# Output stores moved from SyncE to ScalarE and head sums a slot later, in a layer of two token mixers

## The chip, the cores and the metric

The kernel runs on one core of one Trainium2 chip. The metric is the device time of one execution in microseconds, the median of several runs. The engines are named as the profile names them: PE is TensorE (PEld its weight loads), DVE is VectorE, ACT is ScalarE, POOL is GpSimd and SP is SyncE, which here only issues DMAs. DMAs can be issued from SyncE's queue (SPq) or from ScalarE's (ACTq).

## The reference

2048 tokens of 1024 features go through one layer. Cut to what matters:

```python
xn = rms_norm(x, ln_g)
proj = einsum('bsd,de->bse', xn, w_in)
b_gate, c_gate, x_conv, g_conv, x_lru, g_lru = split(proj)      # 1024 columns each
y_conv = short_conv_mixer(b_gate, c_gate, x_conv, conv_w)
y_conv = headwise_rms_norm(y_conv, 8, conv_out_g) * silu(g_conv)
y_lru = rg_lru_mixer(x_lru, ...)                                # gated linear recurrence
y_lru = headwise_rms_norm(y_lru, 16, lru_out_g) * silu(g_lru)
y = concatenate([y_conv, y_lru])                                # 2048 features
h = x + einsum('bse,ed->bsd', y, w_out)
out = rms_norm(h, final_g)
```

The two head-wise norms need, for each token and head, the sum of squares over the head's features: these are the "head sums". The output projection is a product of 2048 features by 1024 columns, and the residual add and the last norm follow row by row.

## The kernel before

**How the products are made.** Every matrix is kept as a high and a low part (`sh`, `sl` for the streaming side, `th`, `tl` for the weights), and each product is three matmuls: `mm` (L877 issues them) takes high by high, high by low and low by high. A Strassen-like scheme needs seven products of half blocks where the plain way takes eight. One half-block product is four chunks `j` of three matmuls, so 12 matmuls of 128x512; such a group is called a **slot** here, and seven (sometimes eight) slots make a **step**. There are 48 steps for the input projection (half `h` of the tokens 0 or 1, block `k` from 0 to 7, and the kinds "l", "a" and "b") and 16 steps "o" for the output projection: phase `ph` 0 and 1, pair of row blocks `m` from 0 to 7.

**What sets the order.** The order is that of the code, engine by engine. `tick()` is called once at the start of each slot; `at(n, f)` puts `f` down to be run `n` ticks later, and whatever it issues stands at that place in the streams of all engines it uses. So "a slot later" means: the instruction stands behind twelve more matmuls on PE, and behind whatever the other engines were given in that slot. Each engine works through its own stream in order, and an instruction that waits holds back all behind it, a DMA issue on SP too.

**The head sums.** `finish` (L560 to L587) is called at the end of a mixer's block. It multiplies with the gate and the gain (`f1`, L565), stores the result to DRAM (`store`, L570), squares it on ScalarE, makes a high part `qh` there (L576) and a low part `ql` on VectorE, and then `head_sums` (L546 to L558) adds up the squares over the features of each head by four small matmuls with a selection matrix `sel`, into the PSUM tile `norm_ps`. After the last block `head_norms` makes the reciprocal roots and stores them (`rsd`). `hl_done(2)` gives two of four tiles of the pool "hl" back to a count, on which a background job (`jobs`, with `may`) hangs: that job prepares the sets `so` of the output projection's streaming side (a ScalarE cast at L417, a VectorE subtraction, a store to DRAM at L422) and the sums `traw` of blocks of `w_out` (loads at L381, stores at L395). Such a job goes on by a piece when the count allows.

**The input projection's copies.** PSUM banks are freed by ScalarE copies: `q` (L1208), `u` (L1211) and `rr` (L1214) take the first three products of a step, and VectorE combines them with later banks. In the kinds "l" ScalarE also starts the convolution, `u<-xl` at L631.

**The output projection.** `outp` (L793 on) makes, for each pair, two row blocks `i` = 0 and 1 of 128 tokens. In phase 0 the first 1024 features of `y` are used: a residual block `xr` is loaded from `x` (L803), the product `ob` added to it on VectorE, and the sum stored to a scratch array `od` in DRAM (L813). In phase 1 the other 1024 features are used: `xr` is loaded back from `od`, added, the row's sum of squares taken on ScalarE (L819) and its root (L820), the block scaled on VectorE (`f2`, L824) and stored to `out` (`f3`, L828). The last block of all (`m` = 7, `i` = 1) goes in two halves (L833 to L841), one store from SP and one from ACT. The weights of a phase are a set of 28 tiles `th`/`tl`; between the phases the second set is loaded (`traw`, L446) and split while the matmuls go on. The streaming sides `s<-so` are loaded at L218.

Of the kernel before, what the change touches and what calls it, by code (L numbers as in the profile page):

```python
# [17 lines left out]
P = 128  # L18
# [20 lines left out]
def hymba_kernel(ctx: ExitStack, tc: tile.TileContext, x, xt, w_in, par, lamc, w_gate, w_out, final_g, out):  # L39
    nc = tc.nc  # L40
# [19 lines left out]
    od = [dram.tile([P, D], F32, name=f"od{b}") for b in range(S // P)]  # L60

    def wt(tag, name, n=2 * C, dt=F32, bufs=1):
        return work.tile([P, n], dt, tag=tag, bufs=bufs, name=name)
# [77 lines left out]
    def at(slots, *fs):  # L141
        if slots == 0:
            for f in fs:
                f()
        else:
            due.append([slots, fs])
# [12 lines left out]
    def tt(out, a, b, op, eng=None):  # L159
        (eng or nc.vector).tensor_tensor(out=out, in0=a, in1=b, op=op)  # L160
# [176 lines left out]
    def hl_tile(name, n=1):  # L337
        hlc[0] += n
        return [wt("hl", name, dt=F32R, bufs=HL) for _ in range(n)]

    def hl_done(n):
        hlc[0] -= n
# [126 lines left out]
    def rstd(rs, ss):  # L469
        nc.scalar.activation(out=rs, in_=ss, func=AF.Sqrt, scale=1.0 / D, bias=eps)  # L470
        nc.vector.reciprocal(out=rs, in_=rs)
# [63 lines left out]
    def head_norms(h):  # L535
        rs = aux("hn")[:R]
        nc.scalar.activation(out=rs, in_=norm_ps[0], func=AF.Sqrt, scale=inv_hd, bias=eps[:R])
        at(1, lambda: nc.vector.reciprocal(out=rs, in_=rs))

        def store():  # L540
            for i in range(2):
                nc.sync.dma_start(rsd[2 * h + i].rearrange("b h t -> h b t"),
                                  rs[32 * i:32 * i + 3 * KT, :].rearrange("h (b t) -> h b t", b=NB))
            normed.extend([h] * h)

        at(3, store)  # L546

    def head_sums(h, qh, ql, col, row):
        if norm_ps[1] == 0:
            norm_ps[0] = psn.tile([P, C], F32, tag="norm", name="norm_ps")[:R]  # L550
        for i in range(2):
            s0 = col - (32 * i + row)
            for q in (qh, ql):
                nc.tensor.matmul(norm_ps[0], sel[:, s0:s0 + R], q[:, i * C:(i + 1) * C],  # L554
                                 start=norm_ps[1] == 0, stop=norm_ps[1] == 8 * KT - 1)
                norm_ps[1] += 1
        if norm_ps[1] == 8 * KT:
            norm_ps[1] = 0  # L558
            at(1, lambda: head_norms(h))

    def finish(d0, h, kt, y, sil, gain, col, row):
        v = {}

        def f1():
            nc.vector.scalar_tensor_tensor(out=sil, in0=y, scalar=gain, in1=sil,  # L565
                                           op0=ALU.mult, op1=ALU.mult)

        def store():
            for i in range(2):
                nc.sync.dma_start(yd[2 * h + i][:, :, kt, :].rearrange("b p t -> p b t"),  # L570
                                  sil[:, i * C:(i + 1) * C].rearrange("p (b t) -> p b t", b=NB))

        def f2():
            nc.scalar.activation(out=y, in_=y, func=AF.Square)
            v["qh"], = hl_tile("qh")
            nc.scalar.copy(v["qh"], y)  # L576

        def f3():
            v["ql"], = hl_tile("ql")
            tt(v["ql"], y, v["qh"].bitcast(F32), ALU.subtract)  # L580

        at(d0, f1)
        at(d0 + 2, store)
        at(d0 + 2, f2)
        at(d0 + 3, f3)
        at(d0 + 6, lambda: head_sums(h, v["qh"], v["ql"], col, row))
        at(d0 + 7, lambda: hl_done(2))  # L587

    def silu(g, late=0):
        sg = [None]  # L590
# [28 lines left out]
    def lru(h, k, late=0):  # L619
# [80 lines left out]
        def out_():  # L700
            finish(0, h, KT + k, v["r"], g, pt[:, LG + k:LG + k + 1], 2 * R, KT + k)
# [20 lines left out]
    def combine(dst, bank, other):  # L722
        if other is None:
            nc.scalar.copy(dst, bank)
        else:
            tt(dst, bank, other, ALU.add)
# [66 lines left out]
    def outp(ph, m):  # L793
        ob = [wt("hl", "ob", bufs=HL) for _ in range(2)]
        xr = {}
        if ph == 1 and m == 0:
            fg[0] = wt("t", "fg")
            nc.sync.dma_start(fg[0], final_g.rearrange("(o d) -> o d", o=1).broadcast_to((P, D)))

        def load(i):  # L800
            tb = 2 * m + i
            xr[i] = wt("ig", "xr", bufs=IG) if i == 0 else wt("o2", "xr", bufs=O2)
            nc.sync.dma_start(xr[i], x[tb * P:(tb + 1) * P, :] if ph == 0 else od[tb])  # L803

        last = ph == 1 and m == KT - 1
        at(2 if last else 5, lambda: load(0))
        at(2 if last else 6, lambda: load(1))

        def fin(i):
            tb = 2 * m + i  # L810
            if ph == 0:
                at(1, lambda: tt(xr[i], xr[i], ob[i], ALU.add))
                at(3, lambda: nc.sync.dma_start(od[tb], xr[i]))  # L813
                return
            ss = small.tile([P, 2], F32, tag="ss", bufs=4, name="ss")
            rs = small.tile([P, 1], F32, tag="rs", bufs=4, name="rs")

            def f1():
                nc.scalar.activation(out=xr[i], in_=ob[i], func=AF.Square, accum_out=rs)  # L819
                nc.scalar.activation(out=rs, in_=rs, func=AF.Sqrt, scale=1.0 / D, bias=eps)  # L820

            def f2():
                nc.vector.reciprocal(out=rs, in_=rs)
                nc.vector.scalar_tensor_tensor(out=ob[i], in0=ob[i], scalar=rs, in1=fg[0],  # L824
                                               op0=ALU.mult, op1=ALU.mult)

            def f3():
                nc.sync.dma_start(out[tb * P:(tb + 1) * P, :], ob[i])  # L828

            if last and i == 1:  # L830
                for d in (1, 0):
                    ds_ = slice(d * C, (d + 1) * C)
                    nc.scalar.activation(out=xr[i][:, ds_], in_=ob[i][:, ds_], func=AF.Square,  # L833
                                         accum_out=ss[:, d:d + 1])
                tt(rs, ss[:, 0:1], ss[:, 1:2], ALU.add)
                rstd(rs, rs)
                for d in range(2):
                    ds_ = slice(d * C, (d + 1) * C)
                    nc.vector.scalar_tensor_tensor(out=ob[i][:, ds_], in0=ob[i][:, ds_], scalar=rs,
                                                   in1=fg[0][:, ds_], op0=ALU.mult, op1=ALU.mult)  # L840
                    (nc.sync, nc.scalar)[d].dma_start(out[tb * P:(tb + 1) * P, ds_], ob[i][:, ds_])  # L841
                return
            if last:
                tt(ob[i], ob[i], xr[i], ALU.add)
                f1()
                f2()
                f3()
                return
            at(1, lambda: tt(ob[i], ob[i], xr[i], ALU.add))
            at(3, f1)  # L850
            at(4, f2)
            at(5, f3)

        def put(which, bank, other):
            i, d = which // 10 - 1, which % 10 - 1
            ds_ = slice(d * C, (d + 1) * C)
            if last and i == 1 and d == 0:
                tt(xr[i][:, ds_], xr[i][:, ds_], other, ALU.add)
                combine(ob[i][:, ds_], bank, xr[i][:, ds_])
            else:  # L860
                combine(ob[i][:, ds_], bank, other)
                if last and i == 1:
                    tt(ob[i][:, ds_], ob[i][:, ds_], xr[i][:, ds_], ALU.add)
            if which == 12:
                fin(0)
            if which == 21:
                fin(1)

        return put
# [41 lines left out]
    with tc.manual_schedule(engines={ENG.PE, ENG.Activation, ENG.DVE, ENG.Pool, ENG.SP}):  # L911
# [173 lines left out]
        for n in range(PLAIN, N):  # L1085
            kind, h, k = steps[n]
# [52 lines left out]
            for s in range(8 if new or last else 7):  # L1139
                i = ((0, 6) + ORDER[1:])[s]  # L1140
# [131 lines left out]
```

## Time and profile before

| | us |
|---|---|
| median of 3 runs | 1426.95 |
| lowest and highest | 1425.71, 1427.22 |
| the profiled execution | 1426.31 |
| its span | 1424.5 |
| PE busy in it | 1335.4 |
| mean granted clock in it | 0.982 of full speed |

The rows of the timeline give the start, the duration, the engine, the line, the operation, the output and input names, and in brackets how long the engine had been idle before it and what ended that. Rows with "x2" join neighbours of one kind. The stages in the table by windows are: a step of the input projection (783 to 841), phase 0 of the output projection without its beginning (1125 to 1253), the passage to phase 1 (1253 to 1282) and phase 1 (1282 to 1405); the rest to 1424.5 is the last block and its norm.

### The profile page before, as it was taken

Reading aid. Unit: us, or ns where it says so; the run is one execution under the profiler, and the core shown is the slowest. Engines: PE = TensorE matmul, PEld = TensorE weight load, DVE = VectorE, ACT = ScalarE, POOL = GpSimd, SP = SyncE. Lnnn points to the kernel's source line nnn. Section 1 sums busy time; section 2 is a strip of 40 time slices with the busy share of each in tenths; the row PEclk is TensorE's granted clock in tenths of the full one; section 3 lists DMA queues with packets and bytes.
Section 4 is the critical chain, followed back from the end, with each engine's and each line's share of the span. In section 5 each row is a group of like instructions: output and inputs, shape, how many; then the busy total and the mean of one; then the engine's idle time right before and its main releaser. Section 6 shows DMA issues by size and latency. Waiting matters only on the chain.

```text
span 1424.5 us, 16977 instructions
## 1 busy us (share of the span) xinstructions
PE 1335.4 (94%) x5732; PEld 1068.4 (75%) x5732; DVE 1069.8 (75%) x1264; ACT 782.0 (55%) x1165; POOL 258.4 (18%) x168
## 2 busy tenths in 40 slices
PE   5979999999999997899998999899996999989997
PEld 4867777778787775677886878687874788868885
DVE  5788887998989889777767667665657548668885
ACT  6576668566665756475563645463646323434442
POOL 2414343434534331001000000101010000000000
PEclk9999999999999998999999999999998999989999
DMA  5137797987978866631899999998978999698643
GB/s 212 30 110 259 271 275 239 284 322 273 328 275 297 305 246 220 225 102 38 276 313 339 332 342 326 347 315 307 288 269 330 348 292 278 215 403 292 216 156 122
DMA packets 165190, 371.02 MB, mean 260 GB/s; under 512 B 17264, under 2 KB 52464, under 8 KB 165104
## 3 DMA queue, kind: packets, MB, share of 16 engines
q1 hardware_dynamic: 164672, 369.63, 75.7%
q8 instruction: 45, 0.74, 0.2%
q14 instruction: 41, 0.34, 0.1%
q10 hardware_dynamic: 432, 0.32, 0.1%
HBM read 224.45 MB, written 145.43 MB: 260 GB/s over the span
## 4 chain that ended last, share of the span: by engine, by line
PE 63%; DVE 11%; DMA 10%; ACT 10%; issue 3%; SPq 2%; POOL 0%; DVEq 0%; ACTq 0%
PE bank L877 59%; DVE s L160 2%; ACT i L668 2%; PE gate L661 2%; DMA traw<-in_w_out_dram 2%; ACT r L668 2%; PE norm_ps L554 2%; DVE tl L160 2%; DMA sd<-s 1%; DVE traw L160 1%; DVE r L695 1%; DMA zr<-rsd 1%; DMA so<-so 1%; DMA s<-sd 1%; ACT q L1208 1%
## 5 line engine op out<-in xcount | busy, mean ns | idle before, releaser
L877 PE MATMUL bank<-th,s 128*128 128x512 f32 x3608 | 1145.6, 394 | 43.1 <-DMA s<-so 8.8
L877 PEld LDWEIGHTS bank<-th,s 128*128 128x128 f32 x3608 | 683.4, 189 | 207.5 <-issue 14.5
L877 PE MATMUL bank<-tl,s 128*128 128x512 f32 x1804 | 709.7, 393 | 7.1 <-DVE tl L160 6.5
L877 PEld LDWEIGHTS bank<-tl,s 128*128 128x128 f32 x1804 | 341.7, 189 | 83.2 <-DVE tl L160 11.7
L160 POOL TENSOR_TENSOR s<-raw,s 128x512 fp32r<-128x512 f32 x67 | 127.2, 1911 | 263.2 <-ACT s L197 217.1
L197 ACT CAST s<-raw 128x512 fp32r<-128x512 f32 x136 | 81.9, 617 | 56.9 <-PE bank L877 39.8
L1211 ACT COPY u<-bank 128x512 f32<-128x512 f32 x58 | 34.0, 587 | 140.1 <-PE bank L877 90.2
L160 POOL TENSOR_TENSOR gb<-gb,sg 128x1024 f32<-128x1024 f32 x16 | 42.5, 2658 | 352.4 <-ACT sg L594 296.1
L160 DVE TENSOR_TENSOR s<-s,s 128x512 fp32r<-128x512 f32 x102 | 100.6, 986 | 5.4 <-ACT s L197 5.4
L160 DVE TENSOR_TENSOR tl<-traw,th 128x512 fp32r<-128x512 f32 x98 | 66.5, 705 | 46.9 <-ACT th L454 29.4
L160 DVE TENSOR_TENSOR s<-raw,s 128x512 fp32r<-128x512 f32 (+1 forms) x115 | 86.6, 777 | 9.9 <-ACT s L197 5.3
L1208 ACT COPY q<-bank 128x512 f32<-128x512 f32 x58 | 33.8, 583 | 83.0 <-PE bank L877 75.8
L160 DVE TENSOR_TENSOR raw<-raw,zr 128x512 f32<-128x512 f32 x64 | 47.9, 769 | 36.8 <-DMA zr<-rsd 36.8
L197 ACT CAST s<-s 128x512 fp32r<-128x512 f32 x102 | 62.8, 616 | 7.5 <-DVE s L160 7.4
L635 DVE SCALAR_TENSOR_TENSOR u<-xl,pt,u 128x1024 f32<-128x1024 f32 x48 | 65.4, 1363 | 0.7 <-ACT u L631 0.2
L1214 ACT COPY rr<-bank 128x512 f32<-128x512 f32 x58 | 33.9, 584 | 45.7 <-PE bank L877 45.6
L745 DVE SCALAR_TENSOR_TENSOR t<-p,pt,t 128x1024 f32<-128x1024 f32 x32 | 48.5, 1517 | 4.9 <-ACT t L742 4.1
L160 DVE TENSOR_TENSOR st<-u,st 64x1024 fp32r<-64x1024 f32 x32 | 50.9, 1590 | 1.0
L160 POOL TENSOR_TENSOR gl<-gl,sg 128x1024 f32<-128x1024 f32 x16 | 45.6, 2849 | 14.4 <-ACT sg L594 14.4
L631 ACT ACTIVATE u<-xl,pt 128x1024 f32<-128x1024 f32 x16 | 19.9, 1246 | 48.1 <-DVE xl L160 48.0
L160 DVE TENSOR_TENSOR ob<-bank,rr 128x512 f32<-128x512 f32 x18 | 12.2, 689 | 44.7 <-ACT rr L1214 44.7
L668 ACT ACTIVATE r<-gate,pt 64x512 f32<-64x512 f32 x64 | 43.7, 683 | 1.7 <-PE gate L661 1.1
(161 smaller groups left out, 1372.2 us busy)
## 6 DMA issues: line engine op xcount, KB each, us to landing
sd<-s SPq DMA_DIRECT2D x147, 512.0 KB, 4.8
s<-sd SPq DMA_DIRECT2D x147, 512.0 KB, 6.0
raw<-in_w_in_dram SPq DMA_DIRECT2D x108, 256.0 KB, 4.7
so<-so SPq DMA_DIRECT2D x42, 512.0 KB, 6.2
s<-so SPq DMA_DIRECT2D x42, 512.0 KB, 7.5
raw<-yd SPq DMA_DIRECT2D x64, 256.0 KB, 5.8
traw<-in_w_out_dram SPq DMA_DIRECT2D x56, 256.0 KB, 5.9
yd<-gl SPq DMA_DIRECT2D x32, 256.0 KB, 3.7
```

Of the source, the lines that this page charges most:

```text
L160: (eng or nc.vector).tensor_tensor(out=out, in0=a, in1=b, op=op)
L197: nc.scalar.copy(dst[i][0], val(i))
L554: nc.tensor.matmul(norm_ps[0], sel[:, s0:s0 + R], q[:, i * C:(i + 1) * C], start=norm_ps[1] == 0, stop=norm_ps[1] == 8 * KT - 1)
L631: nc.scalar.activation(out=v["u"], in_=o1[:, 1:1 + N2], func=AF.Identity, scale=lw[0], bias=pt[:, LB + k:LB + k + 1])
L635: nc.vector.scalar_tensor_tensor(out=v["u"], in0=o1[:, 1 + j:1 + j + N2], scalar=lw[j], in1=v["u"], op0=ALU.mult, op1=ALU.add)
L661: nc.tensor.matmul(ps[j], v["gw"][n][:, j, :], v["st"][j][:, sl], start=(n == 0), stop=(n == 1))
L668: nc.scalar.activation(out=g_[hi, sl], in_=v["ps"][j][src], func=AF.Sigmoid, bias=pt[src, bias + k:bias + k + 1])
L745: nc.vector.scalar_tensor_tensor(out=tcur["t"], in0=p[:, 2 + j:2 + j + N2], scalar=cw[j], in1=tcur["t"], op0=ALU.mult, op1=ALU.add)
L877: nc.tensor.matmul(bank, a[:, js], b, start=start and n == 0, stop=stop and n == 2, skip_group_check=more)
L1208: nc.scalar.copy(q1, bk["A"])
L1211: nc.scalar.copy(u2, bk["A"])
L1214: nc.scalar.copy(rr, bk["A"])
```

## The change

`head_sums` and the `hl_done` behind it come a slot later in every call of `finish`. The stores of phase 0 (16, of 512 KB) and of phase 1 (15, of 512 KB) are issued by ScalarE instead of SyncE, and each a slot later: three slots after the add in phase 0, two slots after the scaling in phase 1. In the last step `f3` is called at once, without `at`, and now goes to ScalarE too.

```diff
@@ finish
-        at(d0 + 6, lambda: head_sums(h, v["qh"], v["ql"], col, row))
-        at(d0 + 7, lambda: hl_done(2))
+        at(d0 + 7, lambda: head_sums(h, v["qh"], v["ql"], col, row))
+        at(d0 + 8, lambda: hl_done(2))
@@ outp, fin
-                at(3, lambda: nc.sync.dma_start(od[tb], xr[i]))
+                at(4, lambda: nc.scalar.dma_start(od[tb], xr[i]))
...
-                nc.sync.dma_start(out[tb * P:(tb + 1) * P, :], ob[i])
+                nc.scalar.dma_start(out[tb * P:(tb + 1) * P, :], ob[i])
...
-            at(5, f3)
+            at(6, f3)
```

Three places show it in the streams. The first is on PE, in a step "l" of the second half, at 774 us of the trace. `norm_ps` are the head sums with `qh` and `ql` (two more, alike, follow the two shown), `bank_6456` and `bank_6354` two PSUM banks, `th` weights and `s` streaming sides. Before:

```order
L877 MATMUL bank_6456<-th_4878,s_6332 128x512
L554 MATMUL norm_ps_5465<-qh_6370,sel_177 64x512
L554 MATMUL norm_ps_5465<-ql_6403,sel_177 64x512
...
L877 MATMUL bank_6354<-th_4743,s_6330 128x512
L877 MATMUL bank_6354<-tl_4744,s_6330 128x512
...
L877 MATMUL bank_6354<-th_4904,s_6330 128x512
L877 MATMUL bank_6456<-th_4626,s_6352 128x512
```

The same place after the change:

```order
L877 MATMUL bank_6456<-th_4878,s_6332 128x512
L877 MATMUL bank_6354<-th_4743,s_6330 128x512
L877 MATMUL bank_6354<-tl_4744,s_6330 128x512
...
L877 MATMUL bank_6354<-th_4904,s_6330 128x512
L554 MATMUL norm_ps_5493<-qh_6370,sel_177 64x512
L554 MATMUL norm_ps_5493<-ql_6403,sel_177 64x512
...
L877 MATMUL bank_6456<-th_4626,s_6352 128x512
```

The head sums have moved behind the twelve matmuls into `bank_6354`, to directly before the first matmul that writes `bank_6456` again. All 32 groups have moved in the same way.

The second place is on ACT, in the last steps of phase 0 and the passage to phase 1, from 1237 to 1255 us in the trace before: the stores of row blocks 12 to 15 among the copies that free banks (`u`, `rr`, `ob`) and the casts of the weights of phase 1 (`th<-traw`).

```order
 L454 CAST th<-traw 128x512 x2
 L197 CAST s<-raw 128x512
-L1211 COPY u_10035<-bank 128x512
+L1211 COPY u_10034<-bank 128x512
+L813 DMA od_148<-xr 128x1024
 L454 CAST th<-traw 128x512 x4
 L1214 COPY rr<-bank 128x512
+L813 DMA od_149<-xr 128x1024
 L454 CAST th<-traw 128x512 x4
 L724 COPY ob<-bank 128x512
-L454 CAST th<-traw 128x512 x18
+L454 CAST th<-traw 128x512 x4
+L813 DMA od_150<-xr 128x1024
+L813 DMA od_151<-xr 128x1024
+L454 CAST th<-traw 128x512 x14
```

`od_148` to `od_151` are the stores of row blocks 12 to 15; the last two stand next to each other. On SP the same four stores are gone from between the loads of `s<-so` and `traw`.

The third place is on ACT at the end of the program: the copies and norms of the last pair of row blocks.

```order
 L820 ACTIVATE rs<-rs,eps 128x1
 L1214 COPY rr<-bank 128x512
-L724 COPY ob<-bank 128x512
-L819 ACTIVATE xr,rs<-ob 128x1024
-L820 ACTIVATE rs<-rs,eps 128x1
+L828 DMA out_dram<-ob 128x1024
+L724 COPY ob<-bank 128x512
+L819 ACTIVATE xr,rs<-ob 128x1024
+L820 ACTIVATE rs<-rs,eps 128x1
+L828 DMA out_dram<-ob 128x1024 x2
 L833 ACTIVATE xr,ss<-ob 128x512 x2
 L470 ACTIVATE rs<-rs,eps 128x1
```

Two stores (row block 14, called at once, and block 13, two slots behind its scaling) now stand between the root of block 14 and the two squares of block 15 (L833).

## The prediction

> **What bounds the kernel now.** The first page of the profile gives the span and each engine's share of it.
>
> ```profile
> span 1424.5 us, 16977 instructions
> PE 1335.4 (94%) x5732; PEld 1068.4 (75%) x5732; DVE 1069.8 (75%) x1264; ACT 782.0 (55%) x1165; POOL 258.4 (18%) x168
> ```
>
> TensorE is busy for 94% of the span. So an edit is worth what it does to TensorE's waits, or to TensorE's rate. The profiled execution took 1426.31 us: 1.8 us lie around its span, and it stands 0.6 us under the median of 1426.95 us. I add my terms to the median. About 0.2% (2.9 us) is what a measurement of this kernel can tell from no change.
>
> Next I read the list of what TensorE waits for, and then the same table for SyncE's DMA queue.
>
> ```profile
> PE bank L877 <- DMA s<-so: 8.8, 5, 3.3
> PE bank L877 <- ACT q L1208: 6.0, 5, 1.4
> PE norm_ps L554 <- DVE ql L160: 5.5, 4, 1.4
> PE bank L877 <- DMA s<-sd: 4.6, 6, 1.0
> ```
>
> ```profile
> SPq L828 <- DVE ob L824: 67.4, 15, 13.6
> SPq L813 <- DVE xr L160: 26.5, 7, 7.1
> ```
>
> The columns are microseconds in all, times, and the longest. The third row of the first table is the wait of the head sums, which the change moves: 5.5 us in four pieces. The two rows below are the waits of the stores that leave SyncE. They are large, but they are waits of a queue, and cost time only where a load behind them comes late for TensorE. Whether one does is read from the busy time by stages: TensorE, its weight loads, VectorE, ScalarE, GpSimd, then granted clock, DMA share and GB/s.
>
> ```profile
> core 0: us, PE busy (x) PEld busy (x) DVE busy (x) ACT busy (x) POOL busy (x), PEclk, DMA share, GB/s
> 783.00:841.00 58.00, 56.49 (x246) 45.38 (x244) 36.50 (x42) 31.09 (x42) 6.31 (x4) 1.00 0.97 339
> 1125.00:1253.00 128.00, 128.00 (x565) 105.67 (x564) 78.30 (x108) 39.78 (x69) 0.00 (x0) 1.00 0.86 279
> 1253.00:1282.00 29.00, 23.14 (x81) 17.74 (x80) 16.33 (x25) 11.04 (x19) 0.00 (x0) 0.82 1.04 401
> 1282.00:1405.00 123.00, 123.00 (x543) 101.55 (x542) 100.53 (x148) 56.66 (x109) 0.00 (x0) 1.00 0.63 214
> ```
>
> The output projection runs from about 1105 us. In 1125 to 1253 (phase 0) and 1282 to 1405 (phase 1) TensorE has no idle time at all. So in 251 of its 320 us the stores and their waits cost nothing today. Only the passage between the phases (1253 to 1282) has idle time and a lowered clock.
>
> **The head sums, a slot later.** I take the first of the four waits apart in the timeline. TensorE:
>
> ```profile
> 774.25 0.40 PE L554 MATMUL norm_ps<-qh,sel 128*64 128x512 f32 x1
> 776.02 0.45 PE L554 MATMUL norm_ps<-ql,sel 128*64 128x512 f32 x1 [1.38 <-DVE ql L160]
> 781.09 0.50 PE L877 MATMUL bank<-th,s 128*128 128x512 f32 x1 [1.41 <-ACT q L1208]
> ```
>
> VectorE and ScalarE in the same stretch:
>
> ```profile
> 774.14 0.69 DVE L160 TENSOR_TENSOR gl<-bank,rr 128x512 f32<-128x512 f32 x1 [6.33 <-DMA yd<-gl]
> 774.75 1.22 DVE L160 TENSOR_TENSOR ql<-r,qh 128x1024 fp32r<-128x1024 f32 x1
> 778.54 0.68 DVE L160 TENSOR_TENSOR xl<-bank,q 128x512 f32<-128x512 f32 x1
> 779.33 1.24 ACT L631 ACTIVATE u<-xl,pt 128x1024 f32<-128x1024 f32 x1 [8.11 <-DVE xl L160]
> 780.47 0.56 ACT L1208 COPY q<-bank 128x512 f32<-128x512 f32 x1
> ```
>
> VectorE stands 6.33 us before `gl` until an earlier store has landed, and everything behind it is late: first `ql`, on which the head sums wait 1.38 us, and then without a pause `xl`, ScalarE's `u` and, queued behind `u`, the copy `q`, which frees the PSUM bank that TensorE wants at 781.09 (again a wait, 1.41 us). Nothing in this second chain depends on the head sums. After the change the twelve matmuls that stood behind the head sums run at 774.25 and the head sums follow, with `ql` (ready at 775.97) no longer waited for. But the bank still comes at 781.09. So the 1.38 us are given back 5 us later, as one gap of 1.38 + 1.41 = 2.8 us. Two more of the four sites have the same second gap:
>
> ```profile
> 846.65 0.50 PE L877 MATMUL bank<-th,s 128*128 128x512 f32 x1 [1.39 <-ACT q L1208]
> 913.26 0.50 PE L877 MATMUL bank<-th,s 128*128 128x512 f32 x1 [1.41 <-ACT q L1208]
> ```
>
> The fourth (974 us) shows no wait of TensorE at its `q`; there up to 1.4 us might stay won, but the weight load stands there already, so I count nothing. Term: 0, bounds -1.4 and 0. The other 28 groups of head sums wait for nothing and only change places.
>
> A gap of 2.8 us is another thing than two of 1.4, since the clock answers to gaps. I look for gaps of nearby size in the timeline of TensorE.
>
> ```profile
> 568.78 0.49 PE L877 MATMUL bank<-th,s 128*128 128x512 f32 x1 [2.06 <-ACT th L277]
> 578.15 0.74 PE L877 MATMUL bank<-th,s 128*128 128x512 f32 x1 [2.57 <-ACT th L277]
> 579.47 1.05 PE L877 MATMUL bank<-th,s 128*128 128x512 f32 x2
> 581.86 0.63 PE L877 MATMUL bank<-th,s 128*128 128x512 f32 x2
> 1254.59 0.47 PE L877 MATMUL bank<-th,s 128*128 128x512 f32 x1 [0.85 <-DMA s<-so]
> 1257.23 0.54 PE L877 MATMUL bank<-th,s 128*128 128x512 f32 x1 [1.71 <-DVE tl L160]
> 1275.42 0.76 PE L877 MATMUL bank<-th,s 128*128 128x512 f32 x1 [3.30 <-DMA s<-so]
> 1281.47 0.63 PE L877 MATMUL bank<-th,s 128*128 128x512 f32 x2
> ```
>
> After 2.06 us of idleness the next matmul takes 0.49 us; after 2.57 and 3.30 us it takes 0.74 and 0.76, and two overlapped ones take 1.05 us where they take 0.63 at full rate. From 578.15 to 581.86 eight matmuls pass in 3.71 us, which need 8 x 0.23 = 1.84 at the full spacing (0.23 us is what a second, overlapped matmul adds: two take 0.63, the single one at 774.25 took 0.40): 1.9 us lost. From 1275.42 to 1281.47 fourteen matmuls lose 6.05 - 3.22 = 2.8 us. Three gaps of 2.8 us, then, above the 2.57 that drops the clock, at 1.9 each: +5.7 us, bounds 0 (no drop) and 3 x 2.8 = 8.4. Part of it is taken back, where TensorE waited for DMA loads between the sites: in that stretch the DMA share is 0.97 (the row of 783 to 841), so a later TensorE finds these loads landed. The `s<-sd` row above holds 4.6 us in all; I let half of the loss be absorbed: +2.9.
>
> [...]
>
> On TensorE, at the first of these sites, the order before has the four head sums (`norm_ps`) ahead of the twelve matmuls into the other bank, and after the change behind them; nothing else moves there. Loads of `xcol` and `xrow` on SyncE that wait for the head sums (in the first 300 us) go 2.7 us later, ahead of a use several microseconds away: 0. Since `hl_done` comes later too, six of the background splits `so` (a ScalarE cast and a VectorE subtraction) stand one slot later and four sets of `w_out` loads two loads later on SyncE. No row of TensorE's waits shows these at the places concerned; I count 0, with 1 us to either side in the range.
>
> **The stores on ScalarE.** One issue costs about the same on either queue:
>
> ```profile
> L828 SPq DMA_DIRECT2D out_dram<-ob x15: 333/338/338, 1292.5 to 1417.0; - x15
> L813 SPq DMA_DIRECT2D od<-xr x16: 319/330/911, 1117.9 to 1257.2; - x16
> 1421.30 0.35 ACTq L841 DMA_DIRECT2D out_dram<-ob x1
> ```
>
> 31 issues x 0.35 = 10.9 us come onto ScalarE. In the two steady stages it works 39.8 + 56.7 = 96 of 251 us, so they hide there; a slot (about 2.7 us) is left between VectorE's result and the store, so ScalarE should hardly wait for VectorE, which would hold back the copies behind the store that free TensorE's banks. SyncE loses its two waits of 67.4 and 26.5 us, but TensorE was waiting for nothing behind them in these stages: 0, not a gain.
>
> What is left is the passage, where TensorE waits for loads that SyncE issues:
>
> ```profile
> 1253.24 0.32 SPq L813 DMA_DIRECT2D od<-xr  x1
> 1254.52 0.32 SPq L218 DMA_DIRECT2D s<-so  x1
> 1268.70 3.09 SPq L218 DMA_DIRECT2D s<-so  x5
> ```
>
> The passage moves 401 GB/s at a DMA share of 1.04: it is bound by transfers. A store of 512 KB takes 0.512 MB / 401 GB/s = 1.3 us of it. The stores of blocks 12 and 13 go some 4 us later, out of a lull before 1235 us into the full time, and those of 14 and 15 stand together on ScalarE at about 1254, on a queue of their own beside the loads. That costs from one to two stores' time, 1.3 to 2.6 us, when the next load is the one TensorE waits for; the third gap, 3.30 us at 1275.42, hangs on loads issued only at 1268.70 and need not move. On the other side the issues leave SyncE's way (0.3 us each) and the loads queued behind them may go earlier: down to -3. I take +1, bounds -3 and +4.
>
> [...]
>
> **The end.** ScalarE now issues the last store of block 14 ahead of its last squares:
>
> ```profile
> 1415.67 1.28 DVE L824 SCALAR_TENSOR_TENSOR ob<-ob,rs,fg 128x1024 f32<-128x1024 f32 x1
> 1415.34 0.61 ACT L833 ACTIVATE xr<-ob 128x512 f32<-128x512 f32 x1
> 1418.38 0.63 ACT L833 ACTIVATE xr<-ob 128x512 f32<-128x512 f32 x1 [2.34 <-DVE ob L160]
> ```
>
> It waits there for VectorE until 1416.95, and two issues of 0.35 us follow (block 13's stands behind it), so the first square starts at about 1417.7 and ends at 1418.5, where the second was to begin at 1418.38: +0.1 to +0.6, taken +0.3.
>
> **The sum.** 0 + 2.9 + 1.0 + 0.3 = +4.2 us on 1426.95: 1431.1, called 1431.0.
>
> **The rivals.** First, no drop of the clock: the merged gaps of 2.8 us fall so that the rate stays full, as after 2.06 us. Then 0 + 0 + 1.0 + 0.3: 1428.3 us, no measurable change. For it: the edge lies between 2.06 and 2.57, and near the edge a gap's place may decide.
>
> Second, faster: SyncE, free of 94 us of waits, feeds the passage earlier. Its three gaps (0.85, 1.71 and 3.30 us) and the 2.8 us lost at half rate behind the last are worth 8.7 us. It decides once the loads land about 1 us sooner: then the last gap falls under the edge of 2.57 us, and I put half of the sum, 4.4 us, as gone: 1426.95 - 4.4 + 0.3 = 1422.9 us if the clock holds at the head-sum sites. Against it: the passage is already full of transfers.
>
> Third, the change of the head sums costs nothing, but blocks 14 and 15 on the second queue hold back the loads of the passage by 2.6 us, and a gap there crosses the edge (1.9 us): 1426.95 + 4.5 + 0.3 = 1431.8. Against it: the third gap takes up part of a delay.
>
> That the change does not do what it says has no chance here: the order has all 32 groups and 31 stores in other places.
>
> **How the numbers follow.** Forecast 0.48, no clock drop 0.27, faster 0.17, transfers 0.08. Of the forecast's case 0.06 falls within 2.9 us of the median, and of the second rival's 0.04 as well when the drop takes part of its gain back; of the no-drop case 0.06 goes below and 0.02 above. Faster: 0.13 + 0.06 = 0.19. Same: 0.06 + 0.19 + 0.04 = 0.29. Slower: 0.42 + 0.02 + 0.08 = 0.52. The forecast's own range is 1428 to 1437: its upper end has the clock's loss unabsorbed (5.7) and the transfers' upper bound (4). For 8 in 10 the lower end goes down to 1423.0, the price of the faster rival, which leaves out its better half.
>
> **What would show it.** Right: TensorE's waits for `ql` at 776, 842, 908 and 974 us gone, a single wait of about 2.8 us for `q` at three of them, then matmuls of 0.74 us and a granted clock under 1.00 for 3 to 6 us; no idle TensorE in the two steady stages; DMA still full in the passage. The no-drop rival: the same gaps, followed by 0.50 us. Wrong: the `q` wait stays at 1.4 us, so that 5.5 us are won; or TensorE waits in the steady stages for copies held behind a store on ScalarE.

## The result and the profile after

The changed kernel takes 1437.31 us (median of four runs, 1435.67 to 1441.15) against 1426.97 us before (four runs, 1425.71 to 1427.22). The ratio is 1.0075 with a 95% interval of 1.0059 to 1.0090: slower by 10.7 us (8.4 to 12.8). The forecast was 1431.0 us with a range up to 1437.0; the direction was right, and the predicted rise of 4.2 us was less than half of what came. The profiled execution is the slowest of the four (1441.15 us, span 1439.2), so its gaps make more than the median shows.

First, where the time went. The copy `rr` (L1214) is made once a step, so the same copy can be looked up in both traces. These are the 30th, 42nd, 45th and last of 58, before:

```profile
763.91 0.59 ACT L1214 COPY rr<-bank 128x512 f32<-128x512 f32 x1
1027.98 0.59 ACT L1214 COPY rr<-bank 128x512 f32<-128x512 f32 x1
1128.47 0.59 ACT L1214 COPY rr<-bank 128x512 f32<-128x512 f32 x1 [5.82 <-PE bank L877]
1406.64 0.59 ACT L1214 COPY rr<-bank 128x512 f32<-128x512 f32 x1 [3.48 <-PE bank L877]
```

and after:

```profile
764.87 0.59 ACT L1214 COPY rr<-bank 128x512 f32<-128x512 f32 x1
1034.70 0.59 ACT L1214 COPY rr<-bank 128x512 f32<-128x512 f32 x1
1141.67 0.59 ACT L1214 COPY rr<-bank 128x512 f32<-128x512 f32 x1 [4.86 <-PE bank L877]
1421.29 0.59 ACT L1214 COPY rr<-bank 128x512 f32<-128x512 f32 x1 [3.48 <-PE bank L877]
```

The lag is 1.0 us at the first, 6.7 at the second, 13.2 at the third and 14.65 at the last. So of the 14.7 us of this pair of executions, 5.8 arise in the stretch with the four head-sum sites, 6.5 from there into the first steps of the output projection, and only 1.5 from there to the end, where nearly all of the 31 stores stand. One pair of executions tells this only roughly: the profile of the run with the phase 0 stores alone (below) lags by 3.5 us at the 44th copy, at 1074 us, ahead of every instruction that it moves. The table by stages, moved by the lag, says the same of the output projection (columns as before; the rows are phase 0, the passage, phase 1):

```profile
1140.00:1267.00 127.00, 127.00 (x561) 104.62 (x559) 77.86 (x108) 39.60 (x68) 0.00 (x0) 1.00 0.84 275
1268.00:1297.00 29.00, 22.41 (x80) 17.58 (x80) 16.34 (x24) 11.52 (x19) 0.00 (x0) 0.82 1.04 401
1297.00:1419.00 122.00, 121.93 (x538) 100.65 (x537) 100.27 (x148) 56.49 (x109) 0.00 (x0) 1.00 0.62 213
```

TensorE is without idle time worth naming in both phases, the passage has the same clock (0.82) and the same transfers (401 GB/s) as before. The list of TensorE's waits shows what has changed:

```profile
PE bank L877 <- DMA s<-so: 11.6, 6, 4.0
PE bank L877 <- ACT q L1208: 11.3, 7, 2.3
PE bank L877 <- DMA s<-sd: 7.1, 6, 2.1
PE bank L877 <- DVE q L160: 6.1, 1, 6.1
PE bank L877 <- DVE gl L160: 2.3, 5, 0.5
```

The head sums' wait for `ql` (5.5 us) is gone from the list. The wait for `q` has grown from 6.0 to 11.3 us, a wait for `gl` has come in (2.3), and one single wait of 6.1 us for a VectorE result `q` is new. The waits for loads (`s<-so`, `s<-sd`) have grown too. The first head-sum site on TensorE, for the rows of 774 to 781 us before:

```profile
776.28 0.50 PE L877 MATMUL bank<-th,s 128*128 128x512 f32 x1 [0.42 <-DVE gl L160]
782.48 0.50 PE L877 MATMUL bank<-th,s 128*128 128x512 f32 x1 [2.25 <-ACT q L1208]
783.04 0.62 PE L877 MATMUL bank<-th,s 128*128 128x512 f32 x2
783.74 1.01 PE L877 MATMUL bank<-th,s 128*128 128x512 f32 x2
784.98 1.05 PE L877 MATMUL bank<-th,s 128*128 128x512 f32 x2
```

The idle time has moved almost whole: 0.42 + 2.25 = 2.67 us where there were 1.38 + 1.41 = 2.79. The first part waits for VectorE's `gl`, which reads the bank that the twelve matmuls, now first in the row, want to write. 1.3 us after the gap the matmuls fall to about half rate (1.05 us for two instead of 0.62); the granted clock is 0.60 in 783 to 787 us. At the fourth site, where TensorE had waited 1.37 us for `ql` and not for `q`, it now waits 0.49 for `gl` and 0.93 for `q`: nothing is won there either. The second great place is the start of the passage into the output projection, on ScalarE:

```profile
1079.03 0.62 ACT L417 CAST so<-raw 128x512 fp32r<-128x512 f32 x1
1081.66 0.60 ACT L417 CAST so<-raw 128x512 fp32r<-128x512 f32 x1
1094.63 0.62 ACT L417 CAST so<-raw 128x512 fp32r<-128x512 f32 x1 [8.38 <-DMA so<-so]
1095.16 1.14 ACT L454 CAST th<-traw 128x512 fp32r<-128x512 f32 x2
```

The third of these casts waits 8.38 us for the landing of an earlier store of `so`, which must free its tile of the pool "hl"; behind it stand the casts of the weights `th`, and VectorE and TensorE hang on these. Before, the same cast waited 3.83 us:

```profile
1081.23 0.62 ACT L417 CAST so<-raw 128x512 fp32r<-128x512 f32 x1 [3.83 <-DMA so<-so]
```

### The profile page after: what moved, and what is told of

The parts are those of the page before. It is cut to its first block, busy times and chain, and to the rows that moved or that the text cites. A ratio compares the mean times of both kernels' runs of the same rounds, so it can differ in the third digit from the quotient of the medians.

```text
span 1439.2 us, 16980 instructions
## 1 busy us (share of the span) xinstructions
PE 1339.7 (93%) x5732; PEld 1072.6 (75%) x5732; DVE 1067.9 (74%) x1264; ACT 782.3 (54%) x1165; POOL 256.9 (18%) x168
## 4 chain that ended last, share of the span: by engine, by line
PE 58%; DMA 14%; DVE 11%; ACT 10%; issue 4%; SPq 1%; POOL 0%; ACTq 0%; DVEq 0%; POOLq 0%
PE bank L877 55%; DMA yd<-gl 3%; DVE s L160 2%; DMA raw<-yd 2%; DMA s<-so 2%; PE gate L661 2%; ACT i L668 2%; PE norm_ps L554 2%; ACT r L668 2%; DMA so<-so 2%; DVE traw L160 1%; DVE tl L160 1%; DMA xcol<-in_xt_dram 1%; DVE r L695 1%; DMA zr<-rsd 1%
## 5 line engine op out<-in xcount | busy, mean ns | idle before, releaser
L1214 ACT COPY rr<-bank 128x512 f32<-128x512 f32 x58 | 33.9, 584 | 46.4 <-PE bank L877 46.4
L160 DVE TENSOR_TENSOR xx<-bank,u 128x512 f32<-128x512 f32 x15 | 10.4, 691 | 52.4 <-PE bank L877 52.4
```

Of the source, the lines that this page charges most:

```text
L1214: nc.scalar.copy(rr, bk["A"])
```

## The experiments

My theory at this point: nearly all of the loss comes from the change in `finish`, by two mechanisms (merged gaps with a falling clock; the splits `so` a slot later, which `hl_done` steers). The rival: the stores on ScalarE. Below, a ratio is always to the kernel before, run beside it on the same chip, and microseconds are that ratio on about 1428 us. The kernel before took 1428.44, 1427.86 and 1429.43 us (medians) beside the three groups of runs, and the ratio is not simply the quotient of the two medians, so a median below is not to be compared with 1426.97.

**The change of `finish` alone.**

```diff
-        at(d0 + 6, lambda: head_sums(h, v["qh"], v["ql"], col, row))
-        at(d0 + 7, lambda: hl_done(2))
+        at(d0 + 7, lambda: head_sums(h, v["qh"], v["ql"], col, row))
+        at(d0 + 8, lambda: hl_done(2))
```

> The change of the head sums and of hl_done alone; the stores stay on SyncE as before. Theory: nearly the whole +10.3 us comes from here, by two mechanisms: merged gaps and clock drops at the four head-sum sites (+2 to +6 us), and the splits `so`, a slot later, whose stores stand behind waiting loads in the passage into the output projection (+5 us). Time 1434 to 1439 us. Rival (the stores on ScalarE cost most of it): 1427 to 1431 us.

Measured: 1437.83 us, ratio 1.0062 (1.0045 to 1.0079), +8.8 us. Most of the loss is here.

**The stores alone.**

```diff
-                at(3, lambda: nc.sync.dma_start(od[tb], xr[i]))
+                at(4, lambda: nc.scalar.dma_start(od[tb], xr[i]))
-                nc.sync.dma_start(out[tb * P:(tb + 1) * P, :], ob[i])
+                nc.scalar.dma_start(out[tb * P:(tb + 1) * P, :], ob[i])
-            at(5, f3)
+            at(6, f3)
```

> The stores on ScalarE, a slot later, alone; head sums and hl_done as before. Theory: 0 to +2 us, 1427 to 1429 us, the passage between the phases some tenths longer. Rival (the stores cost most of it): 1433 us or more.

Measured: 1432.22 us, ratio 1.0017 (1.0004 to 1.0029), +2.4 us. The rival falls as the main cause; a smaller cost of the stores stays, a little above what I expected.

**The head sums late, `hl_done` where it was.** On the other engines the order of the instructions is that of before.

```diff
-        at(d0 + 6, lambda: head_sums(h, v["qh"], v["ql"], col, row))
+        at(d0 + 7, lambda: head_sums(h, v["qh"], v["ql"], col, row))
```

> Only the head sums a slot later, hl_done where it was, so that only TensorE's order changes. Theory: the merged gaps of 2.2 us or more before `q` at 781, 847 and 913 us, with a clock drop after some; the passage before phase 0 as before; +2 to +5 us, 1429 to 1432 us. Rival (the head sums free the tiles of the pool hl later, and that is what delays the splits `so`): a wait of 6 us for `q` in the passage also here, 1434 us or more.

Measured: 1430.16 us, ratio 1.0009 (0.9996 to 1.0022), +1.3 us, not clear of no change. The gaps are those of the changed kernel, and the rate fell at one of the three sites, at 914 us, as TensorE's rows show:

```profile
914.04 0.50 PE L877 MATMUL bank<-th,s 128*128 128x512 f32 x1 [2.26 <-ACT q L1208]
914.37 0.43 PE L877 MATMUL bank<-tl,s 128*128 128x512 f32 x1
914.60 1.05 PE L877 MATMUL bank<-th,s 128*128 128x512 f32 x2
918.01 0.40 PE L877 MATMUL bank<-tl,s 128*128 128x512 f32 x1
```

From 914.60 to 918.01 eight matmuls pass in 3.41 us, where 8 x 0.23 = 1.84 would do: a fall costs some 1.6 us here. By this estimate the two falls in the changed kernel make about half of the 5.8 us that it lost in this stretch.

At 782.68 a gap of 2.25 us was followed by full rate in this execution (0.63 us for two matmuls); the changed kernel's rate fell after the gaps that ended at 782 and 916 us (granted clock 0.64 from 782.5 to 787.2 and 0.59 from 916.2 to 920.4) and not after this one at 849 (1.00 up to 853):

```profile
848.96 0.50 PE L877 MATMUL bank<-th,s 128*128 128x512 f32 x1 [2.23 <-ACT q L1208]
850.23 0.63 PE L877 MATMUL bank<-th,s 128*128 128x512 f32 x2
```

**`hl_done` late, the head sums where they were.** This moves six splits `so` on ScalarE and VectorE, their stores and four sets of `w_out` loads on SyncE; TensorE's order stays.

```diff
-        at(d0 + 7, lambda: hl_done(2))
+        at(d0 + 8, lambda: hl_done(2))
```

> Only hl_done a slot later, the head sums where they were: it moves six splits `so` on ScalarE and VectorE and loads on SyncE. Theory: the passage before phase 0 (1083 to 1130 us) grows by 5 us, with ScalarE waiting some 8 us for the landing of a store of `so`; the four waits for `ql` and those for `q` stay at 1.4 us with no clock drop; 1431 to 1434 us. Rival (delay comes from the head sums): 1426 to 1428 us.

Measured: 1434.06 us, ratio 1.0035 (1.0019 to 1.0050), +5.0 us. This line is the dearest of the change. ScalarE waits 6.77 us for the store of `so`, and TensorE behind it 5.17 us:

```profile
1090.51 0.62 ACT L417 CAST so<-raw 128x512 fp32r<-128x512 f32 x1 [6.77 <-DMA so<-so]
1093.63 0.79 PE L877 MATMUL bank<-th,s 128*128 128x512 f32 x1 [5.17 <-DVE q L160]
```

One thing was not as expected: the rate fell in this execution too, though the head sums stood where they were: behind a wait for `q` of 1.80 us at 848 us two matmuls took 1.05 us (rows in the last section).

**`hl_done` late in one block only**, the convolution of block 6 in the second half, which leaves all as it was but the last of the six places where splits move.

```diff
-        at(d0 + 7, lambda: hl_done(2))
+        at(d0 + (8 if h == 1 and kt == KT - 2 else 7), lambda: hl_done(2))
```

> hl_done a slot later only in the convolution of block 6 of the second half, which moves just the last split `so` (ahead of the passage into the output projection) and its store on SyncE. Theory: this alone makes the passage from 1074 to 1128 us longer by 2.5 to 3.5 us, with ScalarE waiting 8 us for the landing of a store of `so` and TensorE 5 us for `q`; the stretch up to 1048 us stays as before; 1429.5 to 1431.5 us on 1427 to 1428. Rival (the passage is late because all earlier steps are): as before.

Measured: 1432.01 us, ratio 1.0025 (1.0012 to 1.0037), +3.6 us. In the order of each stream no more has moved than one cast, one subtraction and one store of `so` (two neighbouring splits of the job stand a slot later, the first where the second was). ScalarE's wait is there (7.04 us) and TensorE's too, of the same size as with all six:

```profile
1086.57 0.62 ACT L417 CAST so<-raw 128x512 fp32r<-128x512 f32 x1 [7.04 <-DMA so<-so]
1089.69 0.80 PE L877 MATMUL bank<-th,s 128*128 128x512 f32 x1 [5.47 <-DVE q L160]
```

Why the wait grew stands on SyncE. The pool has four tiles, and the cast that waits is the fifth split in a row, so it needs the tile of the first, which is free when that split's store has landed. Before, the store was issued ahead of two loads of weights:

```profile
1073.40 0.42 SPq L422 DMA_DIRECT2D so<-so  x1
1074.41 1.07 SPq L446 DMA_DIRECT2D traw<-in_w_out_dram  x2
```

and here behind them:

```profile
1076.05 1.56 SPq L446 DMA_DIRECT2D traw<-in_w_out_dram  x2
1077.66 0.42 SPq L422 DMA_DIRECT2D so<-so  x1
```

This execution lagged by 1.5 us already (at 1050 us, where nothing differs yet). Beyond that the store is issued 2.8 us later, and the waiting cast starts 3.9 us later (1086.57 against 1081.23), which is about what the run costs.

**`hl_done` late in all other blocks.**

```diff
-        at(d0 + 7, lambda: hl_done(2))
+        at(d0 + (8 if kt != KT - 2 else 7), lambda: hl_done(2))
```

> hl_done a slot later in all blocks but that one. Theory: the passage from 1074 us on as before, and the stretch from 763 to 1048 us longer by 2 to 4 us through waits for loads of `s<-sd` that stand beside the moved loads of `traw`; 1429 to 1431.5 us. Rival: all of the 5 us of the count's shift come back here, 1432 us or more.

Measured: 1430.1 us, ratio 1.0011 (1.0000 to 1.0022), +1.6 us. 3.6 + 1.6 make about the 5.0 of the whole line. The cast in the passage waits 2.48 us here, less than before:

```profile
1083.59 0.62 ACT L417 CAST so<-raw 128x512 fp32r<-128x512 f32 x1 [2.48 <-DMA so<-so]
```

**`hl_done` a slot earlier.**

```diff
-        at(d0 + 7, lambda: hl_done(2))
+        at(d0 + 6, lambda: hl_done(2))
```

> The other way: hl_done a slot earlier, directly behind the head sums, which stand where they stood. Six splits `so` move one slot forward. If the lateness of `so` is what costs, this gains or leaves the time: 1423 to 1427.5 us, with less than 9.8 us of waits of TensorE between 1080 and 1100 us. Rival (any move off the tuned place costs, since the loads then collide): 1430 us or more.

Measured: 1427.7 us, ratio 1.0001 (0.9989 to 1.0013). No gain: TensorE's waits are then for loads, among them 2.99 us for `s<-sd` at 1081 us and 2.83 for `s<-so` at 1094. Standing a slot earlier, the splits win nothing; only a slot later costs.

**The stores of phase 0 alone**, with the first pair of lines of the edit of both phases.

> Only the stores of phase 0 on ScalarE, a slot later. Theory: the cost of the stores, 2.4 us in the run of both phases, lies in the passage between the phases, where the transfers are full, so that it is all here: 1429 to 1431 us. Rival (it lies with the stores of phase 1 and at the end): 1427 to 1428 us.

Measured: 1430.22 us, ratio 1.0018 (1.0003 to 1.0033), +2.6 us.

**The stores of phase 1 alone**, with the other two pairs of lines of that edit.

> Only the stores of phase 1 on ScalarE, a slot later, with the one of the last step ahead of the last squares. Theory: 0 to +0.6 us, all at the end, the steady stage without waits of TensorE: 1427 to 1428.5 us. Rival (the stores on ScalarE hold back the copies that free banks): waits of TensorE between 1300 and 1405 us and 1430 us or more.

Measured: 1428.53 us, ratio 1.0000 (0.9990 to 1.0010), no difference that can be seen. Between 1282 and 1432 us TensorE waits once, 1.29 us for a copy `u` at 1294; the run with `hl_done` a slot earlier, whose stores all stay on SyncE, has 3.89 us there, so the stores are not needed for it. So the cost of the stores, as far as there is one, belongs to phase 0. Its place is not shown: in the profile of the phase 0 stores alone the three gaps of the passage make 1.55 + 1.70 + 3.31 = 6.6 us against 5.9 before, and the lag grows by 0.2 us from the 45th copy to the last. In the profile of both phases' stores the lag does grow by 3.9 us between the copies of 1243 and 1292 us; but in that of the change of `finish` alone, whose stores stay on SyncE, it grows by 4.1 us in the same stretch, so this can't be put down to the stores. What has changed for certain is on SyncE, which now waits for the landing of these stores with loads behind it. The first row is for `xr` (0.2 us before), the second for the weights (0.9 before):

```profile
SPq L803 <- DMA od<-xr: 10.4, 3, 7.3
SPq L446 <- DMA od<-xr: 7.7, 3, 4.2
```

That the loss is by this way is only argued, and the engine was not parted from the slot.

**The whole change with `hl_done` put back.**

```diff
-        at(d0 + 8, lambda: hl_done(2))
+        at(d0 + 7, lambda: hl_done(2))
```

> The whole change, with hl_done put back to its old slot: head sums a slot later, all 31 stores on ScalarE. If the parts add up, 1427 + 1.3 + 2.4 = 1430.7 us (1429 to 1433), the passage before phase 0 as before. Rival (the count costs more in company of the others, so that 7 or 8 us come back): 1428 to 1429.5 us; or (it costs less) over 1433.

Measured: 1432.42 us, ratio 1.0026 (1.0004 to 1.0047), +3.7 us, which is what head sums (1.3) and stores (2.4) make together. Against the whole change 7.0 of the 10.7 us are gone. That is 2 us more than the line costs alone, as the three parts alone make 8.7 us (1.3 + 5.0 + 2.4) and not 10.7; the intervals are wide enough for either.

**A test of what the wait for `q` hangs on.** In the kernel before, two subtractions of weight blocks stand on VectorE between `ql` and `xl`. Here they come a slot later:

```diff
-                if n in (1, 5):
+                if n in (2, 5):
                     sums()
-                if n in (2, 6):
+                if n in (3, 6):
                     more()
```

> On the kernel before, only the sums of the first `w_out` block of each background job a slot later on VectorE, so that two subtractions of `traw` (1.41 us) no longer stand between `ql` and `xl` at the head-sum sites; their stores move with them on SyncE. Theory (the second wait hangs on VectorE's chain and not on the head sums): the waits for `q` at 781, 847 and 913 us fall from 1.4 us to under 0.3, those for `ql` stay at 1.4; 1422 to 1425 us on 1427. Rival (the `q` wait hangs on something else, the bank or the load): the waits for `q` stay, 1427 us or more.

Measured: 1425.32 us, ratio 0.9974 (0.9962 to 0.9987): 3.7 us faster than the kernel before. VectorE, ScalarE and TensorE at the first site:

```profile
775.18 1.22 DVE L160 TENSOR_TENSOR ql<-r,qh 128x1024 fp32r<-128x1024 f32 x1
776.45 0.45 PE L554 MATMUL norm_ps<-ql,sel 128*64 128x512 f32 x1 [1.42 <-DVE ql L160]
777.64 0.68 DVE L160 TENSOR_TENSOR xl<-bank,q 128x512 f32<-128x512 f32 x1
779.57 0.56 ACT L1208 COPY q<-bank 128x512 f32<-128x512 f32 x1
```

`xl` starts 2.46 us after `ql` instead of 3.79, `q` ends at 780.13, and TensorE runs on without a wait there. So the second wait hung on VectorE's chain and not on the head sums.

**The same with the head sums a slot later.**

```diff
-                if n in (1, 5):
+                if n in (2, 5):
                     sums()
-                if n in (2, 6):
+                if n in (3, 6):
                     more()
...
-        at(d0 + 6, lambda: head_sums(h, v["qh"], v["ql"], col, row))
+        at(d0 + 7, lambda: head_sums(h, v["qh"], v["ql"], col, row))
```

> The same, and the head sums a slot later, hl_done where it was. Theory: with the chain to `q` shortened, moving the head sums now saves their wait: a single wait of about 0.8 us for `q` where both together were 2.8, no clock drop at these sites, 1420 to 1424 us. Rival (the waits only move on to the next load): 1426 us or more.

Measured: 1425.97 us, ratio 0.9975 (0.9962 to 0.9987), the same as without. The time I expected did not come: at the first site TensorE waits 0.42 us for `gl` and 0.92 for `q`, in all 1.34 instead of 1.42. The mean granted clock of the profiled execution is 0.982, and was 0.981 without the move.

## Why the prediction was wrong

- **`hl_done` a slot later, "I count 0, with 1 us to either side".** This is the step that failed. Alone the line costs 5.0 us (2.7 to 7.1), and taking it out of the whole change gives back 7.0. I looked among TensorE's waits for rows that name `so` or `traw` at the places the instructions left, and found none; I should have looked where they arrive. The list that I read from had such a row lower down, for the gap at 1087 us, and the same list for ScalarE names the store itself:

```profile
PE bank L877 <- DVE so L160: 2.9, 1, 2.9
ACT so L417 <- DMA so<-so: 18.2, 5, 4.3
```

  The cast that waits for a tile of the pool "hl" stood in the trace before with 3.83 us of waiting, and behind it the casts of the weights for the next phase. With the last place moved, that wait is 7.04 us, and 3.6 us of the time are lost by this alone. The single microsecond that I allowed "in the range" was not in it either: its upper end is 5.7 + 4 us. That the direction came out right is in large part luck, since the dearest line was one that I had put at nothing.
- **The head sums' wait comes back at `q`.** Right: 2.6 to 2.7 us for 2.8, at the three sites. The wait for `gl` in front of it I had not seen: the twelve matmuls that go first write the bank that `gl` reads.
- **A merged gap drops the clock, "+2.9, bounds 0 and 8.4".** The falls are there, the size was too large: gaps of 2.25, 2.23 and 2.21 us, of which two of three dropped the rate in the changed kernel and one of three with the head sums alone, which cost 1.3 us (-0.6 to 3.1). I had taken the gap as 2.8 us and looked for an edge between 2.06 and 2.57. The runs show no such edge: the rate fell after 1.80 us in one of them and stayed full after 2.50 in another (rows in the last section). Even the trace before had half rate behind the gaps of 0.85 and 1.71 us at 1254 and 1257 (granted clock 0.58 from 1257 to 1260), which I showed and did not count:

```profile
1258.00 1.05 PE L877 MATMUL bank<-th,s 128*128 128x512 f32 x2
```

  Nor was half of the loss absorbed in waits for loads: `s<-sd` went from 4.6 us to 5.0 with the head sums alone and to 7.1 in the changed kernel.
- **The stores.** Expected +1.0 in the passage and +0.3 at the end, measured 2.4 (0.6 to 4.1) together. Phase 1 and the end cost nothing that can be measured: from the root of block 14 to the last issue the changed kernel takes 6.25 us and took 6.16, +0.1. The steady stages of the changed kernel stayed without idle time, as predicted. Phase 0 costs 2.6 us (0.4 to 4.7), more than I took, and by a way that stays open. The upper end of my range was 1437.0, with the median at 1437.31: it allowed for the clock and the transfers, not for the count.
- **The rivals.** The faster one (SyncE, free of its waits, feeds the passage earlier) did not happen: the passage has the same 401 GB/s, and SyncE got new waits, for landings. The third, stores that hold back loads of the passage by 2.6 us with a falling clock, did not bring the time: the change of `finish` alone costs 8.8 us without any moved store. As the way of the stores' own 2.4 us it is neither shown nor excluded. The one without a fall of the clock was right at one site of three, and its price left out the count as well.

## What to carry to other kernels

A line that gives back a buffer or a count is part of the schedule: find every instruction that it lets go, follow each to the place where it now arrives, and read there which queue stands still behind it, even where the last engine's list names something else. When a wait is removed by letting other work go first, look for the next thing that the late engine has to deliver: here `ql` was late because all of VectorE was, and what helped was to shorten its chain (two subtractions moved out of the way, 3.7 us). Where a move joins two small idle gaps, look at the rate behind the joined one too: here it fell after three of six such gaps of 2.2 to 2.3 us (the changed kernel and the head sums alone), and a fall cost some 1.6 us by the estimate above.

## What the runs showed of the hardware that was not expected

The rate of TensorE's matmuls fell (1.05 us for two) after single idle gaps of 2.21, 2.25 and 2.26 us and stayed full (0.63) after others of 2.23 and 2.25 us. Other runs widen this. With the whole change and `hl_done` put back, 2.50 us left the rate full:

```profile
845.77 0.50 PE L877 MATMUL bank<-th,s 128*128 128x512 f32 x1 [2.50 <-ACT q L1208]
847.04 0.62 PE L877 MATMUL bank<-th,s 128*128 128x512 f32 x2
```

and with `hl_done` late alone, 1.80 us (behind a gap of 1.40, five microseconds earlier) did not:

```profile
847.90 0.50 PE L877 MATMUL bank<-th,s 128*128 128x512 f32 x1 [1.80 <-ACT q L1208]
849.28 1.05 PE L877 MATMUL bank<-th,s 128*128 128x512 f32 x2
```

So in these executions the length of the one gap, between 1.80 and 2.50 us, did not decide; what did is not shown. At the head-sum sites where it fell, the fall came between at once and 1.4 us after the matmuls had begun again, and lasted 3.4 to 4 us.
